# Two instead of three TensorE heads in the last row of a log-sum-exp kernel, and four equal loads for that row

## The chip, the cores and the metric

One core of a Trainium2 chip. The metric is the device time of one execution in microseconds, median over plain runs; the nine runs of the kernel before in each of the three calls of experiments lie within 0.63, 1.03 and 0.39 us (0.19, 0.31 and 0.12%). "Span" is the time from the first to the last instruction in a trace. "The landing" means, throughout, the moment at which the second row of tile 62 has arrived in SBUF, and "the tail" is the time from there to the start of the final transpose. Both are read from the chain of waits.

## The reference

```python
def reference(x, bias):              # x: 8 x 2048 x 2048 f32, bias: 8 x 256 f32
    B, S, D = x.shape
    H = bias.shape[0]
    Dh = D // H
    x_heads = x.reshape(B, S, H, Dh).transpose(0, 2, 1, 3)
    x_heads = x_heads + bias[None, :, None, :]
    x_tiled = np.repeat(x_heads, 2, axis=2)
    mx = x_tiled.max(axis=-1, keepdims=True)          # ... log-sum-exp over the 256
    lse = mx.squeeze(-1) + np.log(np.exp(x_tiled - mx).sum(axis=-1))
    return lse.astype(np.float32)
```

## The kernel before

x is read once, in 64 tiles of 128 partitions x 2 rows (k = 0, 1) x 2048 columns, that is 8 heads of 256. A head can be summed in three ways:

- on TensorE: bias and x are added in PSUM by matmuls; ScalarE takes the exponential and the sum in one ACTIVATE;
- as exponential in place (ScalarE), then a multiply by exp(bias) with a sum (VectorE);
- as exponential in place, multiplied and folded to 32 columns on GpSimd, with a small last reduction on VectorE.

The last tiles are cut finer than the bulk. `pe` is the number of heads on TensorE, `fold` that on GpSimd; the second entry of tile 63 is its last row.

```python
PROMPT_F2 = dict(pe=2, acc=2, g0=8, late=False, fold=2)
SINGLE_F1 = dict(pe=1, acc=1, g0=8, late=False, fold=1)
TRIPLE = dict(pe=3, acc=3, g0=8, late=False, fold=0)

STAGES = [
    ...                                   # cut: bulk and the stages up to tile 61
    (62, (SINGLE_F1, SINGLE_F1)),
    (63, (PROMPT_F2, TRIPLE)),
]
LAST_COLS = [                             # column pieces of the loads of tile 63
    [(0, 512), (1280, 2048), (512, 1280)],
    [(0, 512), (768, 1280), (1280, 1792), (512, 768), (1792, 2048)],
]

# per piece, in the order of every engine's instructions (cut)
            if h0 < h1 and not m["late"]:
                done = exp_inplace(t, xt[:, k0:k1, h0 * Dh : h1 * Dh], loads[t, k0, c0])
                if hf < h1:
                    for_pool.append(fold(t, k0, hf, h1, sums, done))
            if c0 == 0:
                flush(for_pe)             # ScalarE's sums of the row before
            if not m["late"]:
                for k in range(k0, k1):
                    for h in range(h0, hf):
                        weigh(t, xt[:, k, h * Dh : (h + 1) * Dh], h, sums[:, k, h : h + 1], done)
    ...
    flush(for_pe)
    flush(for_pool)
    finish_last()                         # transpose of all sums, logarithm, store
```

The softmax here doesn't subtract the row's maximum and nothing guards it: scores larger than these inputs give would overflow.

Of the kernel before, what the change touches and what calls it, by code (L numbers as in the profile page):

```python
# [26 lines left out]
PROMPT_F1 = dict(pe=2, acc=2, g0=8, late=False, fold=1)  # L27
PROMPT_F2 = dict(pe=2, acc=2, g0=8, late=False, fold=2)
SINGLE_F1 = dict(pe=1, acc=1, g0=8, late=False, fold=1)
TRIPLE = dict(pe=3, acc=3, g0=8, late=False, fold=0)  # L30
FOLD = 32

STAGES = [
# [1 line left out]
    (54, (MIXED,)),  # L35
    (57, (PROMPT_F1, PROMPT_F1)),
    (62, (SINGLE_F1, SINGLE_F1)),
    (63, (PROMPT_F2, TRIPLE)),
]

LAST_COLS = [
    [(0, 512), (1280, 2048), (512, 1280)],
    [(0, 512), (768, 1280), (1280, 1792), (512, 768), (1792, 2048)],
]


# [520 lines left out]
```

## Time and profile before

| | before |
|---|---|
| plain runs | 327.21 us median (327.03 to 327.37) |
| profiled execution: time, span | 327.84 us, 326.0 us |
| DMA, average over the span | 415 GB/s |
| landing, start of the transpose | 314.48, 322.46 us: a tail of 7.98 us |
| VectorE, ScalarE done with their sums | 321.71, 322.42 us |

In the profile's lines PE is TensorE (PEld its weight loads), ACT ScalarE, DVE VectorE, POOL GpSimd and SPq the queue that issues the loads; L358 is line 358 of the kernel. CUSTOM_DVE_ANT_0 is the trace's name for the multiply with a sum (0.42 us for 256 columns), each followed in the trace by a second, small instruction of 0.08 us, the accumulator read, which writes the sum. The granted clock is the profile's figure for a stretch, as a share of TensorE's full clock. In the chain of waits each line is start, duration and what it was; "issue" is a time in which nothing visible was waited for. The lines themselves are in the prediction.

### The profile page before, as it was taken

How to read it: one execution, taken by the hardware profiler on the slowest of the kernel's cores; microseconds unless marked ns; L12 is line 12 of the kernel's file. 1: busy time of each engine (PE TensorE's matmuls, PEld its weight loads, DVE VectorE, ACT ScalarE, POOL GpSimd, SP SyncE). 2: the span in 40 equal slices, each digit the busy share in tenths (PEclk: the TensorE clock that was granted, in tenths of full speed). 3: DMA queues.
4: the chain of work that ended last, by engine and by line, in shares of the span. 5: the costliest groups of instructions: out<-in, count | busy, mean ns of one | idle time of the engine just before them, and what ended most of it. 6: DMA issues, size and time to landing. Idle time of an engine off the chain costs nothing.

```text
span 326.0 us, 2182 instructions
## 1 busy us (share of the span) xinstructions
PE 263.2 (81%) x565; PEld 90.5 (28%) x565; DVE 283.8 (87%) x306; ACT 263.6 (81%) x425; POOL 290.5 (89%) x123
## 2 busy tenths in 40 slices
PE   4488999599987998878878688688879887498885
PEld 1123333133332333223323223223323222121221
DVE  1005999999999999999989998979998989999994
ACT  1119999489994999698689869879887797999995
POOL 6999999899999999999999999999999899858873
PEclk9999999779995999799799979978997797657755
DMA  8999999999999999999999999999999999999994
GB/s 297 433 428 428 432 424 427 432 420 432 432 422 432 432 417 434 430 420 431 431 422 430 431 422 426 434 422 428 434 424 427 430 426 422 418 423 421 421 387 126
DMA packets 11933, 135.41 MB, mean 415 GB/s; under 512 B 1361, under 2 KB 1745, under 8 KB 2961
## 3 DMA queue, kind: packets, MB, share of 16 engines
q1 hardware_dynamic: 11824, 135.27, 98.7%
q8 instruction: 4, 0.07, 0.1%
q14 instruction: 7, 0.06, 0.0%
q10 hardware_dynamic: 2, 0.01, 0.0%
q0 software_dynamic: 96, 0.00, 0.0%
HBM read 134.23 MB, written 1.05 MB: 415 GB/s over the span
## 4 chain that ended last, share of the span: by engine, by line
DVE 41%; DMA 39%; PE 7%; ACT 6%; POOL 5%; issue 1%; SPq 0%
DVE R L342 36%; DMA xt<-in_x_dram 36%; DVE xt L335 6%; ACT xt L323 4%; PE pair L267 3%; POOL xt L317 3%; DMA b<-bparts 2%; PE one_ps L267 2%; PE pair L249 2%; ACT xt L285 1%; DMA brow<-in_bias_dram 1%; ACT xt L298 1%; POOL brest L173 1%; POOL brest L171 1%; PE pair L231 0%
## 5 line engine op out<-in xcount | busy, mean ns | idle before, releaser
L317 POOL TENSOR_TENSOR xt<-xt,b_rep 128x2048 f32<-128x2048 f32 x57 | 258.7, 4542 | 19.6 <-DMA xt<-in_x_dram 19.6
L342 DVE TENSOR_REDUCE R<-xt 128x14 f32<-128x3584 f32 (+1 forms) x56 | 214.5, 3830 | 1.9
L323 ACT ACTIVATE xt<-xt 128x2560 f32<-128x2560 f32 (+5 forms) x77 | 158.5, 2068 | 10.9 <-POOL xt L317 10.6
L267 PE MATMUL pair<-xt,ident 128*128 128x512 f32 x216 | 116.3, 666 | 0.0
L267 PE MATMUL one_ps<-xt,ident 128*128 128x512 f32 x108 | 65.8, 694 | 21.2 <-DMA xt<-in_x_dram 21.2
L285 ACT ACTIVATE xt<-pair 128x1024 f32<-128x1024 f32 x54 | 56.7, 1050 | 19.9 <-PE pair L267 18.5
L267 PEld LDWEIGHTS pair<-xt,ident 128*128 128x128 f32 x216 | 46.2, 214 | 60.9 <-issue 60.9
L335 DVE TENSOR_TENSOR xt<-xt,w_ps 128x512 f32<-128x512 f32 x54 | 36.7, 681 | 28.0 <-ACT xt L323 27.9
L278 ACT ACTIVATE xt<-one_ps 128x256 f32<-128x256 f32 x108 | 41.1, 400 | 8.1 <-PE one_ps L267 8.0
L249 PE MATMUL pair<-xt,ident 128*128 128x512 f32 (+1 forms) x36 | 30.3, 946 | 7.8 <-DMA xt<-in_x_dram 7.6
L214 PE MATMUL one_ps<-b,ones 3*128 3x512 bf16 x54 | 20.8, 386 | 18.2 <-ACT xt L278 12.1
L214 PEld LDWEIGHTS <-ones 3*128 3x128 bf16 x162 | 13.6, 92 | 71.6 <-issue 65.5
L214 PE MATMUL pair<-b,ones 3*128 3x512 bf16 x108 | 32.3, 378 | 0.0
L267 PEld LDWEIGHTS one_ps<-xt,ident 128*128 128x128 f32 x108 | 17.0, 198 | 44.0 <-DMA xt<-in_x_dram 35.1
L278 ACT ACTIVATION_READ_ACCUMULATOR xt<-one_ps 128x1 f32 x108 | 24.5, 227 | 0.0
L358 DVE CUSTOM_DVE_ANT_0 xt<-xt,w_ps 128x256 f32<-128x256 f32 x61 | 22.4, 418 | 0.0
L382 POOL TENSOR_TENSOR xt<-xt 128x128 f32<-128x128 f32 (+3 forms) x39 | 13.9, 356 | 3.1
L374 POOL TENSOR_TENSOR xt<-xt,w_sb 128x256 f32<-128x256 f32 (+1 forms) x13 | 10.0, 773 | 5.2 <-ACT xt L323 4.5
L298 ACT ACTIVATE xt<-pair 128x256 f32<-128x256 f32 x33 | 12.4, 389 | 0.6 <-PE pair L249 0.6
L249 PEld LDWEIGHTS pair<-xt,ident 128*128 128x128 f32 x36 | 8.2, 278 | 16.7 <-DMA xt<-in_x_dram 13.1
L413 ACT ACTIVATE res<-tpair 64x512 f32<-64x512 f32 x7 | 4.1, 590 | 8.7 <-PE tpair L403 8.5
L358 DVE CUSTOM_DVE_ANT_0 xt<-xt,one_ps 128x256 f32<-128x256 f32 x27 | 10.6, 415 | 0.5 <-ACT xt L323 0.5
(38 smaller groups left out, 60.6 us busy)
## 6 DMA issues: line engine op xcount, KB each, us to landing
xt<-in_x_dram SPq DMA_DIRECT2D x57, 2048.0 KB, 29.1
xt<-in_x_dram SPq DMA_DIRECT2D x12, 1024.0 KB, 24.7
xt<-in_x_dram SPq DMA_DIRECT2D x4, 256.0 KB, 11.4
out_dram<-res SPq DMA_DIRECT2D x1, 896.0 KB, 6.7
xt<-in_x_dram SPq DMA_DIRECT2D x2, 384.0 KB, 15.8
xt<-in_x_dram SPq DMA_DIRECT2D x2, 128.0 KB, 6.3
out_dram<-res_last SPq DMA_DIRECT2D x1, 128.0 KB, 1.7
b<-bparts POOLq DMA_DIRECT2D x3, 1.5 KB, 6.5
```

The source lines that it names most:

```text
L214: nc.tensor.matmul(p, lhsT=ones3, rhs=each_row(b3, h * Dh, Dh, K), start=True, stop=False,)
L249: mm = nc.tensor.matmul(p, lhsT=ident, rhs=xts[t % NBUF][:, ka:kb, c : c + w], start=False, stop=True,)
L267: mm = nc.tensor.matmul(p, lhsT=ident, rhs=xts[t % NBUF][:, :, h * Dh : (h + 1) * Dh], start=False, stop=True,)
L278: act = nc.scalar.activation(out=xts[t % NBUF][:, k, 0:Dh], in_=got[0][:, k * Dh : (k + 1) * Dh], func=ACT.Exp, accum_out=sums[:, k, 0:1],)
L285: act = nc.scalar.activation(out=xts[t % NBUF][:, :, Dh : m["pe"] * Dh].rearrange("p k (h j) -> p h k j", j=Dh), in_=got[-1].rearrange("p ...
L298: act = nc.scalar.activation(out=xts[t % NBUF][:, k, h * Dh : (h + 1) * Dh], in_=p, func=ACT.Exp, accum_out=sums[:, k, h : h + 1],)
L317: add = nc.gpsimd.tensor_tensor(out=v, in0=v, in1=each_row(b_rep, c - G0, D - c, k1 - k0), op=ALU.add)
L323: return on_x(t, nc.scalar.activation(out=v, in_=v, func=ACT.Exp), [after])
L335: mul = nc.vector.tensor_tensor(out=f, in0=f, in1=each_row(w_ps, m["pe"] * Dh - W0, n, k1 - k0), op=ALU.mult,)
L342: red = nc.vector.tensor_reduce(out=sums[:, k0:k1, h0:H], in_=v.rearrange("p k (h j) -> p k h j", j=Dh), op=ALU.add, axis=mybir.AxisListTy ...
L358: ttr = nc.vector.tensor_tensor_reduce(out=v, in0=v, in1=w, scale=1.0, scalar=0.0, op0=ALU.mult, op1=ALU.add, accum_out=dst,)
L382: done = nc.gpsimd.tensor_tensor(out=v[:, :, 0:n], in0=v[:, :, 0:n], in1=v[:, :, n : 2 * n], op=ALU.add)
```

## The change

Its intent: relieve TensorE, which runs without a gap in the tail (314.52 to 321.89 us) at a granted clock of 0.50, by giving it two heads instead of three in the last row, and load that row in four equal pieces, since the third head no longer needs its own.

```diff
-TRIPLE = dict(pe=3, acc=3, g0=8, late=False, fold=0)
+PROMPT = dict(pe=2, acc=2, g0=8, late=False, fold=0)
@@
-    (63, (PROMPT_F2, TRIPLE)),
+    (63, (PROMPT_F2, PROMPT)),
@@
-    [(0, 512), (768, 1280), (1280, 1792), (512, 768), (1792, 2048)],
+    [(0, 512), (512, 1024), (1024, 1536), (1536, 2048)],
```

## The prediction

> **What bounds the kernel now.** I read the page first, then the chain of waits over the last 36 us, then the timeline of each engine and of the DMA queue from 314 us on, because the diff touches only the second row (k = 1) of the last tile (t = 63). Everything before it is issued unchanged. The page has the DMA at 9 tenths in nearly every slice, so up to the last rows the kernel is a stream of x at 415 GB/s; nothing in the diff changes its bytes. The chain shows where the stream stops being the limit:
>
> ```profile
> 294.61 19.87 DMA xt<-in_x_dram
> 314.48 0.04 issue
> 314.52 1.22 PE pair L249 x2
> 315.75 0.53 PE pair L231
> 316.28 2.01 PE pair L249 x2
> 318.29 0.75 PE pair L231 x2
> 319.04 2.02 PE pair L249 x2
> 321.06 0.02 issue
> 321.08 0.84 ACT xt L298 x4
> 321.92 0.01 issue
> 321.93 0.48 ACT xt L298 x2
> 322.42 0.04 issue
> 322.46 0.49 PE tpair L424
> ```
>
> At 314.48 the second row of tile 62 lands. From there TensorE runs without a gap: that row's one head, the bias and two heads of the last tile's first row, the bias of the last row (x2: a 512-column and a 256-column product) and its first two heads. ScalarE then sums those two heads (0.84 us), and the third one (0.48 us), which TensorE has just finished. The transpose at 322.46 waits for all sums. After it come the logarithm, the store and the end at 326.0.
>
> The other engine that must be done by the transpose is VectorE. The end of its timeline, beside TensorE's third head:
>
> ```profile
> 320.80 0.41 DVE L358 CUSTOM_DVE_ANT_0 xt<-xt,w_ps 128x256 f32<-128x256 f32 x1
> 321.14 0.42 DVE L358 CUSTOM_DVE_ANT_0 xt<-xt,w_sb 128x256 f32<-128x256 f32 x1
> 321.49 0.22 DVE L388 TENSOR_REDUCE R_last<-xt 128x2 f32<-128x64 f32 x1
> 321.26 0.63 PE L249 MATMUL pair<-xt,ident 128*128 128x256 f32 x1
> ```
>
> The reader is to see that VectorE has no idle time in this stretch and ends at 321.49 + 0.22 = 321.71, only 0.71 us before ScalarE (322.42). That is all the room there is to gain before the other engine takes over.
>
> [...] the table of stages has a clock of 0.50 in every stage from 308 us on (0.93 for 304 to 308), and a 512-column f32 pass takes 1.06 us there against a mean of 0.67 in the bulk. [...] the trace has 416 to 419 ns for the multiply-and-sum. But they start 0.34 us apart (320.80, 321.14, and the reduction at 321.49), accumulator read included, so 0.34 and not 0.42 is what one more costs. [...] The trace has 0.63, and back to back they start 0.52 apart; I use those. [...]
>
> **The change, part by part.** The last row now has two heads on TensorE instead of three; head 2 goes the way of the others, exponential in place on ScalarE and a weighted sum on VectorE.
>
> - TensorE loses the 256-column bias product and the two passes over head 2. On the chain a 512-column bias alone is 0.53 us (at 315.75) and 512 plus 256 is 0.75, so 0.22 us goes ahead of the first two heads. They then end at 321.06 - 0.22 = 320.84. The passes on head 2, 321.06 to about 321.90, disappear.
> - ScalarE loses the third sum with its accumulator read (0.48 us) at the very end. It gains exponential columns: the pieces were 512, 512 and 256 (320.50 was their end), now 512 three times. They start at 319.05, 319.57 and 320.09, and the last now ends at 320.09 + 0.63 = 320.72. The two sums start when TensorE is ready, about 320.86, and end 0.84 later at 321.70: 0.72 us earlier than now.
> - VectorE gains one multiply-and-sum and its accumulator read: 0.34 us, with nothing taken away. Row k = 1 begins on VectorE at 319.78; six times 0.343 end at 321.84, and the reduction of the folded heads adds 0.22: 321.71 + 0.34 = 322.05. It would only be later if it had to wait for an exponential: head 2 is wanted at 319.78 and its exponential ends at 319.05 + 0.63 = 319.68; head 4 at 320.46 against 320.20; head 6 at 321.15 against 320.72. All hold, the first by only 0.1 us.
> - GpSimd's fold of the first row ends at 321.26 and is untouched.
> - The loads: 1 MB as before, in four pieces of 256 KB instead of three of 256 and two of 128. A load goes out when the eighth before it has landed (my inference: the queue's issues at 302.03, 304.56, 307.01, 309.50, 311.98 and 314.50 coincide with the landings that TensorE waits for one row at a time). One piece fewer means that the last goes out at about 311.98 instead of 314.50 and the store of the first seven batches at 314.5 instead of 315.21. This gains nothing by itself, since the stream is full: the last three pieces land at 309.50 + 9.5 = 319.0, 311.98 + 7.4 = 319.4 and 314.50 + 5.2 = 319.7, in the order of their issue, each a few tenths ahead of ScalarE. By the bytes ahead of them the new third and fourth pieces should land at about 319.0 and 319.7 too, ahead of 319.57 and 320.09.
>
> ```profile
> xt<-in_x_dram SPq DMA_DIRECT2D x1, 256.0 KB, 9.5
> xt<-in_x_dram SPq DMA_DIRECT2D x1, 128.0 KB, 7.4
> xt<-in_x_dram SPq DMA_DIRECT2D x1, 128.0 KB, 5.2
> ```
>
> The sum: the transpose now waits for the later of ScalarE (321.70) and VectorE (322.05). It moves from ScalarE's 322.42 to VectorE's 322.05, some 0.36 us earlier; what follows is unchanged. Of the 0.72 us that TensorE and ScalarE save, half is taken by VectorE. 327.21 - 0.36 = 326.85 us, 0.1% less.
>
> **The rivals.**
> Rival A, the clock of the tail is not always slow. The time is 327.03 to 327.37 in three plain runs and 327.84 in the profiled one, and the clock's state changes from one stage to the next (0.93 in the stage from 304 to 308, 0.50 after). With the full clock in the tail TensorE would be far ahead: about 6.5 us of products from 314.5 on take half, so it ends near 318, and ScalarE can go from its exponentials (320.50) to three sums at 0.36 each, about 321.65, with VectorE's 321.71 as the bound before the change. After it the bound is 322.05 all the same, and the change loses 0.34: about 327.5. For it: nothing but that some executions could be in that state. Against it: the clock is 0.50 in all the last 18 us and in most of 284 to 304[...]. I give it one chance in four.
> Rival B, the full saving: VectorE is hidden and ScalarE stays last, 0.72 us gained, 326.5. Against it is that VectorE shows no idle time from 316.3 us on, so another 0.34 us of work has no gap to go into. One in ten.
> Rival C, the wait moves to the loads: the last piece is twice as large, so its exponential has to wait for 256 KB, and the store, going out 0.7 us earlier, shares the DMA engines with it. If the last piece landed 0.5 us late (320.2 or so, against the 320.09 at which ScalarE wants it), the exponential would end at 320.83 or later and head 6 is wanted on VectorE at 321.15. So this has 0.3 us of slack, and a later landing would cost what is over that. In its favour is that the last DMA stage carries only 258 to 320 GB/s; against it that the last load is asked for 2.5 us earlier. It would give 327.0 to 327.3. One in seven.
>
> **Range and chances.** Weighing 326.85 at about half, 327.5 at a quarter, 326.5 and 327.2 for the rest gives 327.0. The plain runs spread by 0.34 us, and another stretch of runs may differ by as much again, so eight times in ten I expect 326.4 to 327.6. Two per cent is 6.5 us, as much as nearly all the work between the last load and the transpose; neither a gain nor a loss of that size can come out of one head of one row. Hence 0.01, 0.98 and 0.01.
>
> **What would show it.** Right: the chain of waits in the changed kernel ends in VectorE (a multiply-and-sum, then L388) ahead of the transpose, the transpose starts near 322.1 with the second row of tile 62 landing at 314.5 as now; ScalarE's two last sums end near 321.7; TensorE has one bias product and two 512-column passes for the last row; there are six multiply-and-sums on VectorE for it with no idle time between; the store of the first seven batches is issued near 314.5. Wrong: a clock over 0.5 in the tail (rival A); a chain that still ends in ScalarE's L298 (rival B); idle time on ScalarE ahead of L323 put down to a load after 318 us (rival C); or a landing of tile 62's rows that itself has moved by some tenths, which the change gives no reason for.

Passages of it that no trace or run of this case shows are cut, with the cuts marked. The sum stands on the 327.21 us of the plain runs and on times read from the trace of the kernel before, and came to 327.21 - 0.36 = 326.85 us, and weighed with the rivals to 327.0. 416 to 419 ns is one multiply-and-sum of 256 columns on VectorE, and 0.63 us (0.52 from start to start) one exponential of 512 columns on ScalarE. That TensorE's 6.5 us of products "take half" at the full clock was the estimate from the granted clock of 0.50; e12 later had 1.12 and 1.13 us for two 512-column passes at 1.00, where the kernel before and the changed one have 2.08 at 0.50.

## The result, and the profile after

327.52 us median (327.46 to 327.58, 4 runs) against 327.29 us (327.03 to 327.61, 4 runs) of the kernel before: the ratio is 1.0007, 95% interval 0.9989 to 1.0024. That is in the predicted range but 0.5 us over the weighed centre of 327.0 (0.67 over the 326.85 of the sum). Ratios are the mean time of one kernel's fast runs over that of the other's fast runs of the same rounds, so not quite the ratio of the medians quoted.

The chain of waits of the changed kernel, at the tail's beginning and end:

```profile
294.30 19.85 DMA xt<-in_x_dram
314.16 0.02 issue
314.18 1.71 ACT xt L323
315.88 0.02 issue
315.91 0.42 DVE xt L358
...
321.23 0.34 DVE xt L358
321.57 0.01 DVE R_last L358
321.58 0.14 DVE R_last L388
321.72 0.14 issue
321.86 0.46 PE tpair L424
```

TensorE is gone from it. From the landing (294.30 + 19.85 = 314.15) it goes through the 1792-column exponential of tile 62's second row to VectorE, which then works without a pause up to its last reduction (321.72). The tail is 321.86 - 314.15 = 7.71 us, 0.27 less than before. ScalarE, the last one before, is now early; its timeline, with the same columns, ends so ahead of the logarithm:

```profile
318.73 1.67 ACT L323 ACTIVATE xt<-xt 128x512 f32<-128x512 f32 x3
320.54 0.38 ACT L298 ACTIVATE xt<-pair 128x256 f32<-128x256 f32 x1
320.82 0.19 ACT L298 ACTIVATION_READ_ACCUMULATOR xt<-pair 128x1 f32 x1
320.91 0.38 ACT L298 ACTIVATE xt<-pair 128x256 f32<-128x256 f32 x1
321.17 0.20 ACT L298 ACTIVATION_READ_ACCUMULATOR xt<-pair 128x1 f32 x1
```

It is done at 321.37, 7.22 us after the landing, where it took 7.94 before. The DMA queue's timeline shows the last load and the store of the first seven batches:

```profile
311.64 0.33 SPq L141 DMA_DIRECT2D xt<-in_x_dram  x1
314.22 0.72 SPq L417 DMA_DIRECT2D out_dram<-res  x1
```

The last load goes out 2.5 us ahead of the landing and no longer with it (314.50 beside 314.48 before), and takes 7.7 us to land: 319.34, which is 5.19 us after the landing. Before it was 314.50 + 5.2 = 319.7, or 5.2 after. The DMA engines are busy throughout (a share of 1.02 to 1.03 from 312 to 320 us in both traces), and asking earlier brought nothing earlier here.

So the tail is shorter by 0.27 us, as foreseen in kind, but the time does not show it. The experiments ask whether VectorE really sets the new end, which part of the diff does what, and where 0.27 us could go.

### The profile page after: what moved, and what is told of

Its sections match the earlier page's. It is cut to its first block, busy times and chain, and to the rows that moved or that the text cites. A ratio compares the mean times of both kernels' runs of the same rounds, so it can differ in the third digit from the quotient of the medians.

```text
span 325.4 us, 2175 instructions
## 1 busy us (share of the span) xinstructions
PE 257.8 (79%) x562; PEld 88.6 (27%) x562; DVE 284.3 (87%) x308; ACT 264.3 (81%) x423; POOL 290.4 (89%) x123
## 4 chain that ended last, share of the span: by engine, by line
DMA 48%; DVE 35%; POOL 8%; ACT 6%; PE 2%; issue 1%; SPq 0%; DVEq 0%
DMA xt<-in_x_dram 45%; DVE R L342 29%; POOL xt L317 6%; ACT xt L323 5%; DVE xt L335 5%; DMA b<-bparts 2%; DVE xt L358 2%; DMA brow<-in_bias_dram 1%; PE pair L267 1%; PE one_ps L267 1%; POOL brest L171 1%; POOL brest L173 1%; ACT xt L285 0%; PE pair L214 0%; POOL bparts L172 0%
## 5 line engine op out<-in xcount | busy, mean ns | idle before, releaser
L323 ACT ACTIVATE xt<-xt 128x2560 f32<-128x2560 f32 (+4 forms) x77 | 158.4, 2066 | 12.4 <-POOL xt L317 11.9
L267 PE MATMUL pair<-xt,ident 128*128 128x512 f32 x216 | 114.3, 656 | 0.0
L267 PEld LDWEIGHTS pair<-xt,ident 128*128 128x128 f32 x216 | 45.8, 212 | 60.6 <-issue 60.6
L249 PE MATMUL pair<-xt,ident 128*128 128x512 f32 (+1 forms) x34 | 27.6, 907 | 11.2 <-DMA xt<-in_x_dram 11.0
L278 ACT ACTIVATION_READ_ACCUMULATOR xt<-one_ps 128x1 f32 x108 | 23.7, 220 | 0.0
L249 PEld LDWEIGHTS pair<-xt,ident 128*128 128x128 f32 x34 | 7.3, 267 | 19.1 <-DMA xt<-in_x_dram 18.2
```

Source lines behind the costliest of these rows:

```text
L249: mm = nc.tensor.matmul(p, lhsT=ident, rhs=xts[t % NBUF][:, ka:kb, c : c + w], start=False, stop=True,)
L267: mm = nc.tensor.matmul(p, lhsT=ident, rhs=xts[t % NBUF][:, :, h * Dh : (h + 1) * Dh], start=False, stop=True,)
L278: act = nc.scalar.activation(out=xts[t % NBUF][:, k, 0:Dh], in_=got[0][:, k * Dh : (k + 1) * Dh], func=ACT.Exp, accum_out=sums[:, k, 0:1],)
L323: return on_x(t, nc.scalar.activation(out=v, in_=v, func=ACT.Exp), [after])
```

## The experiments

Runs of one call share the runs of the kernel before. Tails are the start of the transpose less the landing in that run's own chain of waits, because the landing itself scatters from 314.10 to 314.64 us over the traces; over all of them the tail of the unchanged program repeats to 0.01 us.

### The changed kernel again, its two halves alone, and a cut exponential

`e1_after` is the changed kernel. `e2_heads` keeps the old pieces, `e3_pieces` the old heads:

```diff
 e2_heads (against the changed kernel)
-    [(0, 512), (512, 1024), (1024, 1536), (1536, 2048)],
+    [(0, 512), (768, 1280), (1280, 1792), (512, 768), (1792, 2048)],
 e3_pieces (against the kernel before)
-    [(0, 512), (768, 1280), (1280, 1792), (512, 768), (1792, 2048)],
+    [(0, 512), (512, 1024), (1024, 1536), (1536, 2048)],
 e4_split (against the changed kernel)
-                done = exp_inplace(t, xt[:, k0:k1, h0 * Dh : h1 * Dh], loads[t, k0, c0])
+                dones = {}
+                for ha, hb in SPLITS.get((t, k0), [(h0, h1)]):   # {(62, 1): [(1, 3), (3, 8)]}
+                    done = exp_inplace(t, xt[:, k0:k1, ha * Dh : hb * Dh], loads[t, k0, c0])
+                    for h in range(ha, hb):
+                        dones[h] = done                           # weigh() waits for dones[h]
```

> The changed kernel again, for a narrow interval. Theory (VectorE takes over at the end): from the landing of tile 62's second row to the start of the transpose 7.70 us against 7.98 before, as in the first two traces, and the time 0.2 to 0.4 us under the kernel before. Rival (the execution's clock state and other scatter are larger than the gain): the same 7.7 us in the trace, but a time within 0.2 us of before, on either side.

> Two TensorE heads in the last row, but still loaded in the old five pieces. Theory: the heads alone do it; VectorE still ends last, transpose 7.6 to 7.8 us after the landing, time equal to the changed kernel within 0.15 us. Rival (the pieces matter: one load fewer in flight order, larger packets): transpose at 7.9 us or later, because head 2's exponential comes as a fourth ACTIVATE and the last load lands later.

> Three TensorE heads as before, the last row in four equal pieces. Theory: ScalarE's third sum still ends last, transpose 7.9 to 8.1 us after the landing, time equal to before within 0.15 us. Rival: a gain of 0.2 us or more from the loads alone.

> The changed kernel with the exponential of tile 62's second row (1792 columns) cut in two, heads 1 and 2 first, so that VectorE need not wait 0.28 us for it ahead of its last uninterrupted run. Theory (VectorE's run of work from there to the end sets the end): the run begins about 0.27 us earlier and the transpose comes 7.4 to 7.5 us after the landing, 0.2 to 0.3 us ahead of the changed kernel, with ScalarE (one ACTIVATE more, about 0.1 to 0.2 us) just behind or level. Rival (something else holds the end): 7.65 to 7.75 as without the cut.

The 0.1 to 0.2 us for one more ACTIVATE is an estimate; the changed kernel's trace has 1536 columns as two exponentials in 1.57 us and as three in 1.67, so 0.10.

| run | tail, us | last ahead of the transpose | median (range), 5 runs | ratio to before (95%) |
|---|---|---|---|---|
| before, of that call | | | 327.49 (327.19 to 327.82), 9 runs | |
| e1_after | 7.71 | VectorE | 327.57 (327.21 to 327.61) | 0.9998 (0.9984 to 1.0012) |
| e2_heads | 7.71 | VectorE | 327.42 (327.26 to 327.76) | 0.9998 (0.9986 to 1.0011) |
| e3_pieces | 7.91 | ScalarE | 327.44 (326.97 to 327.58) | 0.9996 (0.9983 to 1.0008) |
| e4_split | 7.80 | VectorE | 327.54 (327.23 to 327.77) | 1.0000 (0.9988 to 1.0013) |

The heads alone give the whole of the shorter tail, the pieces alone 0.07 us, in an execution in which the first two products after the landing took 1.15 us against 1.22. A higher clock for a part of them is a guess: the clock of that stretch is not on record for e3 (they took 0.70 in e12, at 1.00). In time no run differs from before. So of e1's two theories the rival's numbers came: the tail in the trace, nothing in the time.

e4 missed its number: 7.80 and not 7.4 to 7.5. The cut did start VectorE earlier (315.51, 1.41 us after the landing instead of 1.76), but a reduction further on caught it, as its timeline shows; the bracket is VectorE's idle time before the line and what ended it:

```profile
315.51 0.41 DVE L359 CUSTOM_DVE_ANT_0 xt<-xt,one_ps 128x256 f32<-128x256 f32 x1
...
318.03 0.19 DVE L389 TENSOR_REDUCE R_last<-xt 128x1 f32<-128x32 f32 x1 [0.39 <-POOL xt L383]
```

L389 adds up the head of tile 62's second row that GpSimd folds, and GpSimd finishes no earlier than before: 3.90 us after the landing, where it took 3.79 without the cut. The two halves of the exponential take 1.80 us together instead of 1.71, and GpSimd waits for the second. So the gap of 0.28 us that the cut closed came back as this wait of 0.39 us.

### A control, VectorE's room, and a version with the waits moved

`e5_before` is the kernel before. `e6_before_2more` and `e7_after_2more` add two multiply-and-sums to the last row, into spare tiles, ahead of head 5's own. `e8_ahead` is e4 with the reduction and ScalarE's sums moved:

```diff
 e6_before_2more, e7_after_2more
+            if t == T - 1 and k0 == 1 and c0 <= 5 * Dh < c1:
+                for i in range(2):
+                    ttr = nc.vector.tensor_tensor_reduce(out=spare, in0=xt[:, 1, 5 * Dh : 6 * Dh],
+                        in1=w_ps[:, 5 * Dh - W0 : 6 * Dh - W0], ..., accum_out=spare_sum[:, i : i + 1])
+                    on_x(t, ttr, [done])
 e8_ahead (beside the cut of e4)
-                if t < T - 1 or k0 == 0:
+                if t < T - 1:
                     flush(for_pool)       # tile 62's last reduction goes to the very end
-            if c0 == 0:
+            if t < T - 1 and c0 == 0:
                 flush(for_pe)             # ScalarE's sums of tile 63 after its exponentials
+            if t == T - 1 and k0 == 0 and c0 == 512:
+                for_pe.pop(0)()           # tile 62's sum after the first row's exponentials
```

> The kernel before once more, as a run of its own, for a second trace of it and as a control of the timing. Theory: the transpose again 7.95 to 8.0 us after the landing of tile 62's second row, with ScalarE last, while the landing itself may lie some tenths earlier than the 314.48 of the first trace; the time equal to the kernel before within 0.1 us. Rival: another end of the chain or a tail shorter than 7.9 us, which would mean that the first trace was no fair sample.

> Kernel before with two more multiply-and-sums on VectorE in the last row, into spare tiles (0.34 us each, results unchanged). Theory: VectorE has 0.7 us of room behind ScalarE, so it ends 0.68 later, just level; the transpose comes 8.0 to 8.1 us after the landing (at most 0.1 later than before) and the time is unchanged within 0.15 us. Rival (VectorE's work is on the path in both kernels, or in neither): as much longer as the changed kernel gets from the same addition.

> Changed kernel with the same two multiply-and-sums more. Theory: VectorE sets its end, so all of 0.68 us shows: transpose 8.35 to 8.45 us after the landing instead of 7.70, time 0.6 to 0.7 us over the changed kernel and about as much over the kernel before less its gain. Rival: under 0.2 us more.

> Changed kernel, with what made VectorE wait or ScalarE busy at the wrong moment moved: the cut of tile 62's second-row exponential, the reduction of its folded head at the very end instead of in the middle (where the cut alone waited 0.39 us for GpSimd), and ScalarE's sums of TensorE heads after the last exponentials. Theory: VectorE's 16 multiply-and-sums then run without a wait and end 7.2 us after the landing, ScalarE's sums at about 7.25; transpose at 7.35 to 7.5 us, 0.2 to 0.35 less than the changed kernel, the span that much shorter. Rival (the exponentials now wait for loads, or a sum for TensorE): 7.6 us or more.

| run | tail, us | last | median (range), 5 runs | ratio to before (95%) | mean span, us | time less span, us |
|---|---|---|---|---|---|---|
| before, of that call | | | 327.61 (326.70 to 327.73), 9 runs | | 325.60 | 1.80 to 1.83 |
| e5_before | 7.97 | ScalarE | 327.63 (327.53 to 327.72) | 1.0007 (0.9994 to 1.0020) | 325.82 | 1.74 to 1.83 |
| e6_before_2more | 8.28 | VectorE | 328.26 (328.06 to 328.59) | 1.0027 (1.0015 to 1.0040) | 326.12 | 2.15 to 2.19 |
| e7_after_2more | 8.51 | VectorE | 328.28 (328.03 to 328.33) | 1.0025 (1.0012 to 1.0039) | 326.34 | 1.87 to 1.93 |
| e8_ahead | 7.51 | GpSimd, then VectorE's last reduction | 327.18 (327.03 to 327.60) | 0.9997 (0.9985 to 1.0010) | 325.32 | 1.83 to 2.10 |

A span is recorded to 0.1 us, so a single difference of time and span is good to 0.05 us.

The control holds. In the tails VectorE's room is plain: the same addition costs the kernel before 0.30 us (7.98 to 8.28) and the changed one 0.80 (7.71 to 8.51). Each addition was larger than foreseen. In the kernel before the two start 0.46 us apart, and so does what follows:

```profile
320.60 0.41 DVE L507 CUSTOM_DVE_ANT_0 spare<-xt,w_ps 128x256 f32<-128x256 f32 x1
...
321.06 0.42 DVE L507 CUSTOM_DVE_ANT_0 spare<-xt,w_ps 128x256 f32<-128x256 f32 x1
...
321.52 0.42 DVE L361 CUSTOM_DVE_ANT_0 xt<-xt,w_ps 128x256 f32<-128x256 f32 x1
```

With 0.92 us put in and 0.30 coming out, 0.62 us were hidden in the kernel before: its room of 0.71 us less about 0.1, the longer hand-over from VectorE to TensorE (below). In the changed kernel 0.81 was put in (0.46 and 0.35) and 0.80 came out. This shows that VectorE sets the changed kernel's end, and did not set the old one's.

But the times say something else: e6 and e7 are level, 328.26 and 328.28. So e7's time came as expected, 0.65 us over before, and e6's did not: it was to be unchanged within 0.15 us. In the kernel before the time is 1.8 us over the span in every run; in e6 it is 2.17, in e7 1.9. Part of the time lies outside what the trace covers, and it is not the same for all these programs. e1's, e2's and e4's means are 1.94, 2.01 and 1.92 against 1.79 for e3 and for the kernel before in that call, and the changed kernel's first four runs had 2.07.

e8 reached 7.51 us, just outside the 7.35 to 7.5 that it was to reach. VectorE's multiply-and-sums ran without a wait, but VectorE sat idle for 0.10 us ahead of its last reduction, until GpSimd had folded the last tile's heads (POOLq is a drain; in the changed kernel it lasts 0.69 us, from 320.56 to 321.25, and GpSimd's last addition, 320.60 to 320.92, runs under it). So GpSimd had become the last:

```profile
320.14 0.46 POOL xt L383
320.59 0.04 issue
320.63 0.63 POOLq L569
321.26 0.02 issue
321.29 0.23 DVE R_last L389
```

By this chain what VectorE waited for came at 321.26, 7.12 us after the landing; in the changed kernel GpSimd's last addition ended 6.76 us after it. Of these 0.36 us 0.10 was there at the end of the addition before (6.46 us after the landing instead of 6.36); the rest lies in the last addition and the drain over it, and why is not shown. e8 has the shortest tail, 0.47 us below the kernel before, and its mean span is the shortest of this call; in time it is 0.9997, not told apart from before.

### What lies outside the span, and the tail with a faster clock

`e9_before_4rows` and `e10_after_4rows` add four tiny memsets to VectorE's start, where it waits anyway (4.31 us, from 1.13 to 5.44 us in the kernel before). They make VectorE's program as long as in e6 (317 instructions in the trace, 7 waits and drains included) and e7 (319). `e11_before_warm` and `e12_after_warm` fill TensorE's waits ahead of the tail (and add two memsets on GpSimd for the operands). That this would raise the clock was a guess, which the two runs test:

```diff
 e9_before_4rows, e10_after_4rows
     nc.vector.memset(ones3, 1.0)
+    for _ in range(4):
+        nc.vector.memset(spare, 1.0)                   # 1 x 128
 e11_before_warm, e12_after_warm, ahead of each bias product of tiles 57 to 62
+                for _ in range(WARM.get(m["pe"], 0) if m["fold"] == 1 else 0):   # {1: 6, 2: 2}
+                    mm = nc.tensor.matmul(p, lhsT=warm_l, rhs=warm_r[:, 0 : rows * w],
+                                          start=True, stop=True)   # bf16, overwritten by the bias
+                    on_bank(bank, mm)
```

> Kernel before with four tiny memsets more on VectorE at its very start, where VectorE has nothing to do: 317 VectorE instructions in the trace, as in the kernel before with two more multiply-and-sums. It is to explain why the time less the span was 1.80 us in all runs of the kernel before, 1.9 to 2.1 in the changed one and 2.17 with two more multiply-and-sums. Theory (the part of the time outside the span depends on how long VectorE's program is, not on how the kernel ends): span as before, 325.5 to 325.9, time less span 2.1 to 2.2, so a time 0.3 to 0.4 over before with the same tail. Rival (it depends on the tail): 1.80, time as before.

> Changed kernel with the same four memsets: 319 VectorE instructions, as in the changed kernel with two more multiply-and-sums. Theory: span and tail as in the changed kernel (transpose 7.65 to 7.75 us after the landing), time less span 1.85 to 1.95, so if anything a little faster than the changed kernel. Rival: 1.95 to 2.1 as in the changed kernel without them.

> Kernel before with idle TensorE time ahead of the tail (tiles 57 to 62) filled by discarded bf16 products, to have the clock at full rate when the tail begins. Theory (the old tail is ScalarE waiting for a half-rate TensorE): with the clock at 1.0 at least for the first part of the tail the third sum comes earlier and the transpose 7.35 to 7.7 us after the landing instead of 7.95, with VectorE (7.25) last in the best case. Rival: still 7.9 to 8.0 with the clock up. If the clock stays at 0.5 the run tells nothing.

> Changed kernel with the same filling. Theory (VectorE ends it whatever the clock): transpose 7.65 to 7.75 us after the landing as without; so with the full clock the change would lose what it gains with the half one. Rival: it comes down along with TensorE.

| run | tail, us | median (range) | ratio to before (95%) | mean span, us | time less span, us |
|---|---|---|---|---|---|
| before, of that call | | 327.70 (327.53 to 327.92), 9 runs | | 325.89 | 1.73 to 1.86 |
| e9_before_4rows | 7.97 | 327.71 (327.17 to 327.85), 5 runs | 0.9996 (0.9984 to 1.0009) | 325.44 | 2.11 to 2.22 |
| e10_after_4rows | 7.70 | 327.42 (327.27 to 327.69), 5 runs | 0.9992 (0.9978 to 1.0006) | 325.52 | 1.89 to 1.97 |
| e11_before_warm | 7.90 | 326.89 (326.71 to 327.54), 4 runs | 0.9978 (0.9965 to 0.9992) | 325.23 | 1.74 to 1.83 |
| e12_after_warm | 7.70 | 327.69 (327.43 to 327.80), 4 runs | 0.9998 (0.9984 to 1.0012) | 325.55 | 2.03 to 2.20 |

The part outside the span followed the length of VectorE's program, whatever the tail did: 317 instructions give 2.16 us on average with the old tail (e9) and 2.17 with a longer one (e6); 319 give 1.92 (e10) and 1.91 (e7). With 313 it is 1.78 to 1.82 on average (the kernel before, e3, e11), with 315, the changed kernel's number, 1.92 to 2.10 (after, e1, e2, e4, e8, e12). It is not monotonic, and with 315 the single runs lie anywhere from 1.76 to 2.20. TensorE's length does not do it: e11 has 32 products more than the kernel before and stands at 1.78. That the two instructions more of the change itself cause its shift is argued from e9 and e10; no run has the old tail with 315. What happens in that time no trace here shows.

The prediction for e9's time, 0.3 to 0.4 us over before, did not come: its spans are 0.45 us shorter than those of the kernel before beside it (325.44 against 325.89), with the same tail. Spans of one program scatter from 325.0 to 325.7 us in its five runs. So whether the longer outside part adds to the time, or is partly given back within the span, is open.

The filling lifted the clock: from 308 to 312 us it is 1.00 in the traces of e11 and e12, beside 0.50 and 0.60 in those of e9 and e10 of the same call, and the mean over the span is 0.904 to 0.928 in their eight runs, beside 0.876 to 0.896 in the nine of the kernel before. Of the two traced executions it held beyond 316 us only in that of e12, as the table of stages shows (stage and length, busy time and count of PE, PEld, DVE, ACT and POOL, then granted clock, DMA share and GB/s; first e11, then e12):

```profile
312.00:316.00 4.00, 3.07 (x13) 1.40 (x13) 3.34 (x20) 3.93 (x7) 2.67 (x7) 0.80 1.02 393
316.00:320.00 4.00, 4.00 (x7) 1.36 (x7) 3.95 (x24) 4.00 (x14) 3.60 (x6) 0.50 1.03 326
```

```profile
312.00:316.00 4.00, 3.06 (x14) 1.47 (x13) 3.32 (x20) 3.92 (x7) 2.65 (x7) 1.00 1.03 395
316.00:320.00 4.00, 1.83 (x4) 0.39 (x3) 3.97 (x24) 4.00 (x13) 3.61 (x6) 1.00 1.03 353
```

For the changed kernel this settles it: TensorE's products of the last row ended at 318.71, 4.4 us after the landing instead of 6.4, and the tail is 7.70 as ever. For the kernel before, the traced execution fell back to 0.50 from 316 us on and its tail is 7.90, so the full-clock tail is not traced. Its other three runs have spans of 325.1, 325.1 and 324.9 us at mean clocks of 0.92 to 0.93, against 325.8 at 0.904 for the traced one. That fits a tail some 0.5 us shorter, as it would be if VectorE were last, but it is an inference: the clock is a mean over the whole span, and the unchanged kernel had a span of 324.9 us too, once in the call of e5, at a mean clock of 0.895. e11 is the only version that is faster than the kernel before with an interval clear of 1, by 0.2%, 4 runs on one chip; it was not repeated.

## Why the prediction was right or wrong

**Which engine ends the tail: right.** VectorE was to end 322.05 - 314.48 = 7.57 us after the landing. It ended 321.72 - 314.15 = 7.57 after it. Its extra 0.34 us, the lack of any idle time to hide it and the six multiply-and-sums are in the trace, and e6 against e7 shows the room before and its absence after.

**ScalarE and TensorE: right.** ScalarE was to be done 321.70 - 314.48 = 7.22 us after the landing, and was (7.22). TensorE lost the two passes and the small bias product, and the chain no longer contains it.

**Loads: right.** The store was issued at 314.22, with the landing, the last load 2.5 us earlier (at 311.64, with the landing of tile 62's first row, whose product starts at 311.67), and neither had an effect. Rival C did not occur: the last piece landed 5.19 us after the landing, as expected from the bytes ahead of it. e2 shows that the old pieces give the same tail.

**The gain of 0.36 us in the tail: mis-sized.** "It moves from ScalarE's 322.42 to VectorE's 322.05, some 0.36 us earlier; what follows is unchanged." The last clause failed. TensorE starts the transpose 0.04 us after ScalarE's last accumulator read but 0.14 us after VectorE's last reduction, in the traces of both kinds of end. So 0.37 became 0.27. In these traces TensorE waits for VectorE in an instruction of its own (an EVENT_SEMAPHORE, 321.75 to 321.80 in the changed kernel) and for ScalarE in the weight load itself (at 322.46 in the kernel before); whether the 0.10 us belong to that wait or to VectorE was not tested.

**From the tail to the time: the step that did not hold up.** The working subtracted the tail's gain from the measured time, taking the rest of the program for fixed. It was not: the changed kernel's time less its span is 1.9 to 2.1 us on average instead of 1.8. In the call of e1 the mean span fell by 0.16 us (325.68 to 325.52), the time less the span rose by 0.15 (1.79 to 1.94), and the mean times are level (327.47 and 327.46). e9 and e10 show that such a shift came with the length of VectorE's program and not with the tail (2.16 and 1.92 us outside the span, at tails of 7.97 and 7.70). That it took the gain is not shown: in e9 the shift was larger, 0.35 us, and the time stayed level. Over three calls the changed program (with four memsets in the third) stood at 1.0007, 0.9998 and 0.9992, each with an interval of about 0.0014 to 0.0018 to either side, 0.5 to 0.6 us. The whole 0.27 us would be a ratio of 0.9992, which lies inside all three. So the times neither show the gain nor exclude it, and where it went, if it went, stays open.

**Rival A: the clock, half shown.** It said the end after the change would not depend on the clock: e12 shows that, at a granted clock of 1.00 up to 320 us. It said the kernel before would end earlier at full clock, so that the change would lose: the spans and times of e11 speak for it, its trace does not show it. In the traces of the first result the tail was at 0.50 in both kernels, so the clock is not what kept the measured time up there; that its number, 327.5, came is a coincidence. Rival B fell with the first trace.

The range held because it had been drawn for this scatter, and by 0.08 us; its centre was 0.5 us too low.

## What to carry to other kernels

Before taking work off the engine that ends last, look at when the second one ends and where the work will go: here 0.72 us left ScalarE's end, 0.34 of it was put on an engine with 0.71 us of room, and no more than 0.37 could remain. Measure a tail from the event that begins it within the same trace, because that resolves 0.01 us where whole times resolve half a microsecond. And a gain of that size has to be looked for in the time as well as in the trace, since the part of the time outside the trace changed here with four tiny memsets more on VectorE (from 1.81 us to 2.16 in the call of e9).

## Other times measured on the way

- Time less the span: 1.8 us with 313 VectorE instructions, about 2.0 with 315, 2.16 to 2.17 with 317 and 1.91 to 1.92 with 319.
- A multiply-and-sum of 256 columns on VectorE: 416 to 419 ns; its accumulator read: 82 ns. One more in a row cost 0.34 us, the accumulator read included.
- After a sum into the spare tile of e6 the next operation started 0.46 us after it, both times; in e7 it was 0.46 and 0.35 us. Why is not shown.
- From one engine's last result to the start of TensorE's transpose: 0.04 us after ScalarE's accumulator read, 0.14 us after VectorE's reduction, with the open point named above.
- An exponential of 512 columns on ScalarE: 0.63 us alone, 0.52 from start to start.
- The clock: in the tail of the kernel before, TensorE's products run without a gap from 314.52 to 321.89 us, and the granted clock is 0.50 in both stages from 316 to 324 us. So being busy for 7.4 us by the profile's count did not raise it there; what does is not shown. With four to twelve discarded 128 x 128 bf16 products a tile it was 1.00 from 308 to 312 us (0.50 in the kernel before, 0.65 in the changed one).
